# A hybrid SSD and latent-attention step on one core: the page table read whole and early, value weights split a head ahead, values three blocks behind scores, the normalisation later, and long GpSimd products in four pieces

## The chip, the core and the metric

The kernel runs on one core of one Trainium2 chip. The core has five engines with a program each: TensorE (PE; its weight loads, which overlap it, are shown as PEld), VectorE (DVE), ScalarE (ACT), GpSimd (POOL) and SyncE (SP), which issues most of the DMAs. They meet only at semaphores. The metric is the device time of one execution in microseconds (us); less is better.

## What is computed

One inference step of a two-layer decoder trunk: a Mamba-2 layer (SSD), then a multi-head latent attention layer (MLA), each with a residual, and a last RMSNorm. There are two groups of tokens: a prompt of 1024 tokens, and a sample group of 8 sequences with 8 new tokens each and 2048 past tokens in a paged cache. The change lies in the MLA layer, which is cut here to what matters:

```python
def latent_partial(q_lat, q_pe, ckv, kpe, mask):
    s = (einsum('bqhc,bkc->bhqk', q_lat, ckv) + einsum('bqhr,bkr->bhqk', q_pe, kpe)) * MLA_SCALE
    if mask is not None:
        s = where(mask, s, NEG_INF)
    m = max(s, axis=-1)
    p = exp(s - m[..., None])
    return m, sum(p, axis=-1), einsum('bhqk,bkc->bhqc', p, ckv)

# prompt: 16 heads, causal attention of 1024 tokens over themselves
# sample: 8 sequences x 16 pages of 128 tokens, gathered through page_table,
#         running maximum and sum over the pages, then
out = einsum('bhqc,chv->bqhv', acc / l[..., None], w_uv)      # 64 values a head
y   = einsum('bte,ed->btd', out * silu(gate), w_out)
```

Products are done in three passes: each fp32 operand x is split into a rounded half `hi` and the rest `lo = x - hi`, and PE forms hi·hi + lo·hi + hi·lo.

## The kernel before

**Stages.** The SSD layer takes about the first 1090 us and is not touched. Then follow, in the MLA layer: the input products with the gates (to about 1205 us), the latent keys and the query latents (to 1280), the queries `pq` (to 1386), among which head 0's keys, values and maxima are worked in; the sixteen prompt heads (`mla_heads`, 1386 to 1774); and the sample group with the output product (`mla_sample`, to the end). PE and POOL run in the order in which `mla_heads` and `mla_sample` are written; the order of ACT, DVE and SP everywhere, and of all engines before the heads, is chosen by a scheduler that simulates the program. Every engine runs its own list strictly in that order.

**A split** (`split`, L128 to L131) is a copy of the source to `hi` on ACT (L130) and the subtraction `lo` (L131) on DVE, or on POOL where the call says so.

**A head** is 12 blocks of keys by queries (four for the first 512 queries, eight for the second). A block t has scores on PE (`qk`, tile `st`, L1728 to L1735), two exponentials on ACT (`th`, rounded, L1739; `P`, exact, L1740), and `tl = P - th` on POOL, or on DVE for each fourth block (L1742). Its values follow (`pv`, L1759 to L1761: `th` by `Vh`, `th` by `Vl`, `tl` by `Vh`), two blocks later: `held` keeps the blocks between, and `LEAD = 2` sets the distance. Between scores and values stand `units` of preparation: the maxima `sc` of the next head (`maxpass`; DVE takes the maximum), and keys `kp`, queries and values of the head after that (`prep`). After the last block of a half the result is normalised: logarithm and exponential on ACT (`rl`), times the gate on DVE (L1771), times `rl` on POOL (`og`, L1773), and a store.

**Every fourth head** the preparation starts with `prep_group`: the weights of four heads' keys and values are loaded (L1580, L1582; tiles `w`), split with `lo` on POOL, and eight products `vp` with the latents `kvh`, `kvl` make the values `Vh`, `Vl` of four heads. For heads 0 to 3 this happens among the queries.

**The page table.** `gather_kpe` (L1835 on, around 1102 us) reads it as one column `kpidx` and gathers the rotary keys. `Sample.__init__`, which is written after the queries, reads it once more, in four DMAs whose elements of 4 bytes each are copied to 32 partitions (`ptab`, L1866), with a column `pslot` (L1868), and three small DVE instructions (L1870 to L1873) make the row numbers `ptidx` of the latent cache.

**The sample group** goes through 32 steps (8 sequences, 4 groups of 4 pages; `flow`, L2106 on): PE transposes a gathered tile `pgr` (`ct`), forms the scores (`sc`), DVE and ACT the softmax with a running maximum (`mn`, `P`, `ln`), PE transposes `P` (`pt`) and multiplies by the latents' halves `kvh`, `kvl`, DVE adds to the accumulator `ac`. `kvl` is one POOL instruction on 128x1024 elements (L2028). The output product of the prompt (`out.pieces`) is woven into these steps; its weights are split in `weight_split` (L2196 on), with three of the `lo` halves `w5l` on POOL at 128x1024 (L2203), and each of its tiles ends in a scaling of `h` on DVE (L2271). The first 11 steps' worth of `flow` run within the last head.

## Time and profile before

| | us |
|---|---|
| median of three runs (2057.29, 2059.13, 2059.75) | 2059.13 |
| the profiled execution: time | 2057.51 |
| the profiled execution: span of its instructions | 2055.7 |
| PE busy in the span (93%) | 1917.0 |
| DVE, ACT, POOL busy | 1172.9, 1108.1, 826.8 |
| mean granted TensorE clock (1.0 is full) | 0.97 |

The rows of the timeline read: start, duration, engine, line, operation, output<-input with the tiles' names, partitions x elements; in square brackets stands how long the engine was idle before the instruction, and what released it. A line such as `PE vp L89 <- DVE ptf L1871: 17.0, 1, 17.0` is a row of the waits: who waited for whom, total, times, longest.

### The profile page before, as it was taken

What the parts mean: (1) busy time and instruction counts of PE and PEld (TensorE: products, weight loads), DVE (VectorE), ACT (ScalarE), POOL (GpSimd) and SP (SyncE); (2) the same over time, 40 slices, a digit from 0 to 9 for tenths busy, and PEclk for the clock granted to TensorE, in tenths of its full rate; (3) what the DMA queues carried; (4) which work ended last, traced back from release to release, by engine and by line L of the source; (5) the groups of instructions that cost most, each with busy time, mean ns of one, the idle gap of its engine ahead of it and who ended that gap; (6) DMA issues with size and microseconds to landing.
All of it is one profiled execution on the core that took longest, in us unless ns stands there. A gap on an engine that the chain in (4) does not pass through costs nothing.

```text
span 2055.7 us, 33651 instructions
## 1 busy us (share of the span) xinstructions
PE 1917.0 (93%) x11953; PEld 1746.7 (85%) x11953; DVE 1172.9 (57%) x2540; ACT 1108.1 (54%) x2603; POOL 826.8 (40%) x1042
## 2 busy tenths in 40 slices
PE   6989999999999999899999999698989999889998
PEld 5879999999999998777788998697878787678887
DVE  4427675757575666545335134466666666666665
ACT  5446666666666666543335224336667677645552
POOL 0317373636455575331000012005454556755541
PEclk9989999999999999899999999899999999899999
DMA  4113323233333333453446321322111112544441
GB/s 147 41 37 91 91 82 93 88 92 92 90 95 88 87 96 120 163 182 126 172 154 198 142 74 50 97 85 64 43 54 38 43 43 84 159 158 127 145 150 38
DMA packets 186351, 206.43 MB, mean 100 GB/s; under 512 B 23068, under 2 KB 151848, under 8 KB 185800
## 3 DMA queue, kind: packets, MB, share of 16 engines
q1 hardware_dynamic: 181352, 185.27, 29.2%
q0 software_dynamic: 4752, 18.88, 2.8%
q8 instruction: 95, 1.56, 0.3%
q14 instruction: 72, 0.59, 0.1%
q10 hardware_dynamic: 80, 0.13, 0.0%
HBM read 150.92 MB, written 53.15 MB: 99 GB/s over the span
## 4 chain that ended last, share of the span: by engine, by line
PE 70%; DVE 7%; DMA 6%; issue 5%; ACT 5%; POOL 5%; SPq 1%; POOLq 0%; DVEq 0%; ACTq 0%
PE pj L89 21%; PE pj L101 8%; PE pq L101 4%; PE pob L101 4%; PE poa L101 4%; PE py L759 3%; POOL kvl L2028 2%; PE o L1761 1%; PE vp L89 1%; PE pz L101 1%; PE pk L101 1%; DMA tkr<-kpe_dh 1%; PE st L1728 1%; PE p L101 1%; PE st L1729 1%
## 5 line engine op out<-in xcount | busy, mean ns | idle before, releaser
L89 PE MATMUL pj<-xh,wih 128*128 128x384 f32 (+1 forms) x768 | 254.5, 335 | 9.0 <-ACT xh L236 4.6
L89 PE MATMUL pj<-xl,wih 128*128 128x384 f32 (+1 forms) x768 | 254.0, 331 | 0.0
L89 PE MATMUL pj<-xh,wil 128*128 128x384 f32 (+1 forms) x768 | 252.2, 329 | 0.0
L1742 POOL TENSOR_TENSOR tl<-P,th 128x384 fp32r<-128x384 f32 (+1 forms) x144 | 134.4, 941 | 133.2 <-ACT P L1740 109.7
L131 DVE TENSOR_TENSOR wil<-wraw,wih 128x512 fp32r<-128x512 f32 x88 | 70.6, 805 | 160.5 <-ACT wih L130 160.3
L89 PEld LDWEIGHTS pj<-xh,wih 128*128 128x128 f32 x768 | 145.4, 190 | 10.6 <-ACT xh L236 5.6
L89 PEld LDWEIGHTS pj<-xl,wih 128*128 128x128 f32 x768 | 146.0, 190 | 0.6
L89 PEld LDWEIGHTS pj<-xh,wil 128*128 128x128 f32 x768 | 145.7, 190 | 0.0
L796 POOL TENSOR_TENSOR y<-y,xD 128x256 f32<-128x256 f32 x64 | 83.7, 1309 | 151.5 <-DVE y L795 141.1
L1739 ACT ACTIVATE th<-st 128x512 fp32r<-128x512 f32 x192 | 94.2, 491 | 91.4 <-PE st L1735 57.9
L101 PE MATMUL pj<-wih,xh 128*128 128x256 f32 x504 | 143.4, 288 | 0.0
L101 PE MATMUL pj<-wil,xh 128*128 128x256 f32 (+1 forms) x504 | 139.1, 282 | 0.0
L617 DVE SCALAR_TENSOR_TENSOR acc<-raw,vec,acc 128x1112 f32<-128x1112 f32 x84 | 130.3, 1552 | 0.2
L101 PE MATMUL pj<-wih,xl 128*128 128x256 f32 x448 | 126.5, 282 | 0.0
L131 POOL TENSOR_TENSOR xddl<-xdd,xddh 128x256 fp32r<-128x256 f32 x64 | 64.0, 1000 | 117.1 <-ACT xddh L130 117.1
L2028 POOL TENSOR_TENSOR kvl<-pgr,kvh 128x1024 fp32r<-128x1024 f32 x32 | 78.0, 2436 | 75.1 <-ACT kvh L2027 75.1
L130 ACT CAST Ch<-acc 128x128 fp32r<-128x128 f32 x56 | 16.9, 302 | 155.9 <-PE py L89 155.9
L734 ACT ACTIVATE M<-M,tok 128x128 f32<-128x128 f32 (+1 forms) x288 | 90.5, 388 | 10.7 <-DMA M<-acs_d 10.6
L101 PEld LDWEIGHTS pj<-wih,xh 128*128 128x128 f32 x504 | 96.0, 191 | 0.0
L101 PEld LDWEIGHTS pj<-wil,xh 128*128 128x128 f32 (+1 forms) x504 | 93.1, 185 | 0.6
L1740 ACT ACTIVATE P<-st 128x512 f32<-128x512 f32 x192 | 93.2, 486 | 0.0
L1761 PE MATMUL o<-tl,Vh 128*128 128x512 f32 x192 | 71.4, 372 | 17.4 <-POOL tl L1742 14.1
(980 smaller groups left out, 6317.7 us busy)
## 6 DMA issues: line engine op xcount, KB each, us to landing
wraw<-in_ssd_w_in SPq DMA_DIRECT2D x92, 256.0 KB
M<-acs_d SPq DMA_DIRECT2D x64, 256.0 KB
y_d<-xD SPq DMA_DIRECT2D x64, 128.0 KB
s<-in_state_ssm SPq DMA_DIRECT2D x32, 256.0 KB
out_s_ssm<-s SPq DMA_DIRECT2D x32, 256.0 KB
wraw<-in_ssd_w_out SPq DMA_DIRECT2D x16, 512.0 KB
q_d<-qt SPq DMA_DIRECT2D x32, 192.0 KB
qp<-q_d SPq DMA_DIRECT2D x8, 768.0 KB
```

Source lines behind the costliest of these rows:

```text
L89: nc.tensor.matmul(out, a, b, start=(i == 0), stop=(i == n - 1))
L101: nc.tensor.matmul(o, a, b, start=(j == 0), stop=(j == len(ops) - 1))
L131: (eng or nc.vector).tensor_tensor(lo, src, hi.bitcast(F32), op=ALU.subtract)
L617: nc.vector.scalar_tensor_tensor(acc, self.raw[bi][:, j : j + n], k.convw[j][:, blk : blk + 1], acc, op0=ALU.mult, op1=ALU.add)
L734: nc.scalar.activation(M[:m, h, :m], M[:m, h, :m], AF.Relu, bias=c.tk[:, 0, 4 * g + h : 4 * g + h + 1], scale=-1.0)
L759: nc.tensor.matmul(py[:m, h * 64 : h * 64 + 64], c.M[:m, h, :m], c.xdt[:m, h * 64 : h * 64 + 64], start=True, stop=True)
L796: nc.gpsimd.tensor_tensor(y[:m], y[:m], c.xD[:m], op=ALU.add)
L1739: nc.scalar.activation(th[:, :n], ps[:, :n], AF.Exp, scale=SCALE)
L1740: nc.scalar.activation(P[:, :n], ps[:, :n], AF.Exp, scale=SCALE)
L1742: eng.tensor_tensor(tl[:, :n], P[:, :n], th[:, :n].bitcast(F32), op=ALU.subtract)
L1761: nc.tensor.matmul(po[:, o:], va, tl[:, :n], start=False, stop=(jb == nj - 1))
L2028: nc.gpsimd.tensor_tensor(rl, raw, rh.bitcast(F32), op=ALU.subtract)
```

## The change

It has five parts.

1. The page table is read in `gather_kpe`, right behind `kpidx`, in one DMA of the whole table to every partition; four casts pick each quarter's columns, and `ptidx` is made there. `Sample.__init__` only takes it over.
2. The value weights have a function of their own, `prep_v`, called in the preparation of the last head of a group for the next group (for group 0 in `prep_group` as before), and both `lo` halves of the weights are made on DVE.
3. `LEAD` is 3, so that values come three blocks behind scores; `tl` gets a fourth buffer.
4. The last product of the normalisation and its store are put off: `pv` returns them as `close`, which `mla_heads` calls two blocks later.
5. `kvl` and the three `w5l` of POOL are done in four instructions on 128x256 elements each.

```diff
-LEAD = 2
+LEAD = 3
...
+        if h % 4 == 3 and h + 1 < MH:
+            yield from self.prep_v(h // 4 + 1)
 
     def units(self, h):
-        return 4 + 10 * (h % 4 == 0)
+        return 4 + 10 * (h % 4 == 0) + 2 * (h % 4 == 3 and h + 1 < MH)
+
+    def prep_v(self, hg):
+        k, w8 = self.k, self.w8
+        k.nc.sync.dma_start(w8[1], self.wuv[:, 256 * hg : 256 * hg + 256].rearrange("(k p) e -> p k e", p=128))
+        yield
+        split(k, *w8[6:], w8[1])
+        yield
...
-        raw, wv = w8[1], w8[6:]
-        nc.sync.dma_start(raw, self.wuv[:, cs].rearrange("(k p) e -> p k e", p=128))
+        wv = w8[6:]
+        if hg == 0:
+            for _ in self.prep_v(0):
+                pass
         yield
-        split(k, *self.wk, self.wkr, nc.gpsimd)
-        split(k, *wv, raw, nc.gpsimd)
+        split(k, *self.wk, self.wkr)
...
-        tl = sp.tile([128, 512], F32R, tag="tl", name="tl", bufs=3)
+        tl = sp.tile([128, 512], F32R, tag="tl", name="tl", bufs=4)
...
-        nc.gpsimd.tensor_tensor(og[pj], og[pj], rl[pj], op=ALU.mult)
-        nc.sync.dma_start(k.og_d[pr, pj, cs], og[pj])
+        def close():
+            nc.gpsimd.tensor_tensor(og[pj], og[pj], rl[pj], op=ALU.mult)
+            nc.sync.dma_start(k.og_d[pr, pj, cs], og[pj])
+        return close
...
+            if len(closing) and closing[0][0] <= 12 * h + t:
+                closing.pop(0)[1]()
             if len(held) > LEAD:
-                hd.pv(*held.pop(0))
+                c = hd.pv(*held.pop(0))
+                if c:
+                    closing.append((12 * h + t + 2, c))
...
 def gather_kpe(k, pool):
...
+    pt = pool.tile([128, NB * NPG], mybir.dt.int32, name="ptab")
+    nc.sync.dma_start(pt, I["page_table"].rearrange("b p -> (b p)").partition_broadcast(128))
+    ps = pool.tile([128, 1], F32, name="pslot")
+    nc.sync.dma_start(ps, I["c_slot"])
+    pf = pool.tile([128, 32], F32, name="ptf")
+    for j in range(4):
+        r = slice(32 * j, 32 * j + 32)
+        nc.vector.tensor_copy(pf[r], pt[r].rearrange("p (q j) -> p q j", j=4)[:, :, j])
+    nc.vector.tensor_scalar(pf, pf, 32.0, ps, op0=ALU.mult, op1=ALU.add)
+    k.ptidx = k.cm.tile([128, 32], mybir.dt.int32, name="ptidx")
+    nc.vector.tensor_copy(k.ptidx, pf)
...
 class Sample:
     def __init__(self, k, pool):
         nc, I = k.nc, k.I
         self.k, self.sp = k, None
-        pt = pool.tile([128, 32], mybir.dt.int32, name="ptab")
-        for j in range(4):
-            src = I["page_table"].rearrange("b (q j) -> j (b q)", j=4)[j : j + 1].to_broadcast([32, 32])
-            nc.sync.dma_start(pt[32 * j : 32 * j + 32], src)
...
-        self.idx = pool.tile([128, 32], mybir.dt.int32, name="ptidx")
-        nc.vector.tensor_copy(self.idx, pf)
+        self.idx = k.ptidx
...
-        nc.gpsimd.tensor_tensor(rl, raw, rh.bitcast(F32), op=ALU.subtract)
+        for r in range(4):
+            nc.gpsimd.tensor_tensor(rl[:, r], raw[:, r], rh[:, r].bitcast(F32), op=ALU.subtract)
...
-        (nc.gpsimd if x & 2 else nc.vector).tensor_tensor(lo, raw, hi.bitcast(F32), op=ALU.subtract)
+        for c in (slice(256 * j, 256 * j + 256) for j in range(4)) if x & 2 else (slice(0, D),):
+            (nc.gpsimd if x & 2 else nc.vector).tensor_tensor(lo[:, c], raw[:, c], hi[:, c].bitcast(F32), op=ALU.subtract)
```

Lines below `LEAD` are numbered higher in the changed kernel. How the engines' lists change at three places:

DVE among the queries, first before. `cqs` is the scaled query latent of the last (64-token) tile, `cql` its `lo` half, L113 the sum that ends that tile; `qt`, `u`, `w_147..` with `cost` and `sint` are the rotary parts of queries that are stored.

```order
L1459 TENSOR_TENSOR cqs_14663<-cqp_14658,vec 128x512
L1486 TENSOR_TENSOR u_14770<-qt_14755,cost 128x128
L1487 TENSOR_TENSOR w_14771<-qt_14755,sint 128x128
L1488 TENSOR_TENSOR qt_14755<-u_14770,w_14771 128x4x16
L1489 TENSOR_TENSOR qt_14755<-u_14770,w_14771 128x4x16
L1870 CAST ptf<-ptab 128x32
L131 TENSOR_TENSOR cql<-cqs_14663,cqh 128x4x128
L1486 TENSOR_TENSOR u_14792<-qt_14777,cost 128x128
L1487 TENSOR_TENSOR w_14793<-qt_14777,sint 128x128
L1488 TENSOR_TENSOR qt_14777<-u_14792,w_14793 128x4x16
L1489 TENSOR_TENSOR qt_14777<-u_14792,w_14793 128x4x16
L113 TENSOR_TENSOR pq_14684<-pq_14684,pq_14667 64x512
```

The same place after the change, where `w_14736` and `w_14740` are the `lo` halves of the key and value weights:

```order
L1459 TENSOR_TENSOR cqs_14675<-cqp_14670,vec 128x512
L131 TENSOR_TENSOR w_14736<-w_14733,w_14735 128x512
L1486 TENSOR_TENSOR u_14782<-qt_14767,cost 128x128
L1487 TENSOR_TENSOR w_14783<-qt_14767,sint 128x128
L131 TENSOR_TENSOR w_14740<-w_14734,w_14739 128x512
L131 TENSOR_TENSOR cql<-cqs_14675,cqh 128x4x128
L1488 TENSOR_TENSOR qt_14767<-u_14782,w_14783 128x4x16
L1489 TENSOR_TENSOR qt_14767<-u_14782,w_14783 128x4x16
L1486 TENSOR_TENSOR u_14804<-qt_14789,cost 128x128
L1487 TENSOR_TENSOR w_14805<-qt_14789,sint 128x128
L113 TENSOR_TENSOR pq_14696<-pq_14696,pq_14679 64x512
```

The cast of the page table is gone from between `cqs` and `cql`, and two `lo` halves that stood on POOL have come in. The page table's six DVE instructions now stand near 1106 us, here as a piece of the difference (`hl` is the `lo` half of the layer's normalised input, `ck6l` and `ck7l` are weights'):

```order
 L237 SCALAR_TENSOR_TENSOR hl<-xtp_7_12971,vec,hh 128x384
+L1869 CAST ptf<-ptab 32x32 x4
+L1870 TENSOR_SCALAR ptf<-ptf,pslot 128x32
+L1872 CAST ptidx<-ptf 128x32
+L237 SCALAR_TENSOR_TENSOR hl<-xtp_0_13043,vec,hh 128x320
 L131 TENSOR_TENSOR ck6l<-wraw,ck6h 128x288
-L237 SCALAR_TENSOR_TENSOR hl<-xtp_0_13043,vec,hh 128x320
-L131 TENSOR_TENSOR ck7l<-wraw,ck7h 128x288
```

They come ahead of an `hl`, which PE's next products read, and one weight's `lo` half moves behind it.

PE at the start of the heads, before: `o_0` are the values of the first head's first block, `st_0_3` the scores of its fourth, `sc` products for the maxima of the second head.

```order
L1695 MATMUL sc_20_15866<-kTh_14729,qTh_14736 128x384
L1759 MATMUL o_0_15869<-th,Vh_14717 128x512
L1760 MATMUL o_0_15869<-th,Vl_14718 128x512
L1761 MATMUL o_0_15869<-tl,Vh_14717 128x512
L1728 MATMUL st_0_3_15875<-qTh_14733,kTh_13521 128x128
L1729 MATMUL st_0_3_15875<-qTl_14734,kTh_13521 128x128
L1730 MATMUL st_0_3_15875<-qTh_14733,kTl_13522 128x128
L1735 MATMUL st_0_3_15875<-mr 128x128
L1695 MATMUL sc_30_15886<-kTh_14729,qTh_14736 128x512
L1695 MATMUL sc_40_15890<-kTh_14729,qTh_14736 128x512
```

After:

```order
L1704 MATMUL sc_20_15866<-kTh_14741,qTh_14748 128x384
L1737 MATMUL st_0_3_15869<-qTh_14745,kTh_13533 128x128
L1738 MATMUL st_0_3_15869<-qTl_14746,kTh_13533 128x128
L1739 MATMUL st_0_3_15869<-qTh_14745,kTl_13534 128x128
L1744 MATMUL st_0_3_15869<-mr 128x128
L1704 MATMUL sc_30_15880<-kTh_14741,qTh_14748 128x512
L1704 MATMUL sc_40_15884<-kTh_14741,qTh_14748 128x512
L1768 MATMUL o_0_15887<-th,Vh_14729 128x512
L1769 MATMUL o_0_15887<-th,Vl_14730 128x512
L1770 MATMUL o_0_15887<-tl,Vh_14729 128x512
```

The fourth block's scores and two products of the next head's maxima now come ahead of the first values.

POOL in the last head, where the sample group's work starts, before (`tk` is a cast of gathered rotary keys, on 96 partitions):

```order
L1773 TENSOR_TENSOR og_20236<-og_20236,rl_1_20237 64x512
L1742 TENSOR_TENSOR tl<-P,th 128x256
L1742 TENSOR_TENSOR tl<-P,th 128x128
L1945 CAST tk_20297<-tkr_20012 96x512
L2028 TENSOR_TENSOR kvl<-pgr_20008,kvh 128x1024
L1742 TENSOR_TENSOR tl<-P,th 128x512
L1773 TENSOR_TENSOR og_20348<-og_20348,rl_0_20349 64x512
L1742 TENSOR_TENSOR tl<-P,th 128x512 x2
```

After:

```order
L1751 TENSOR_TENSOR tl<-P,th 128x256
L1751 TENSOR_TENSOR tl<-P,th 128x128
L1966 CAST tk_20289<-tkr_20004 96x512
L2050 TENSOR_TENSOR kvl<-pgr_20000,kvh 128x256 x4
L1784 TENSOR_TENSOR og_20256<-og_20256,rl_1_20257 64x512
L1751 TENSOR_TENSOR tl<-P,th 128x512 x3
```

`kvl` is in four, and the `og` of the head before has moved from ahead of two `tl` to behind `kvl`.

More of the change, by code (lines that the diff above doesn't have):

```diff
@@ L1788, in mla_heads @@
     k.tc.keep_in_program_order(k.nc.scalar.preload_act_table_set("natural_log_exp_and_others"))
-    held, carry = [], None
+    held, closing, carry = [], [], None
     def step(g):
@@ L1827, in mla_heads @@
                 step(ready)
+            if len(closing) and closing[0][0] <= 12 * h + t:
+                closing.pop(0)[1]()
             if len(held) > LEAD:
-                hd.pv(*held.pop(0))
+                c = hd.pv(*held.pop(0))
+                if c:
+                    closing.append((12 * h + t + 2, c))
     for x in held:
-        hd.pv(*x)
+        c = hd.pv(*x)
+        if c:
+            closing.append((0, c))
+    for _, c in closing:
+        c()
     return flow
@@ L1862, in __init__ @@
         self.k, self.sp = k, None
-        pt = pool.tile([128, 32], mybir.dt.int32, name="ptab")
-        for j in range(4):
-            src = I["page_table"].rearrange("b (q j) -> j (b q)", j=4)[j : j + 1].to_broadcast([32, 32])
-            nc.sync.dma_start(pt[32 * j : 32 * j + 32], src)
-        ps = pool.tile([128, 1], F32, name="pslot")
-        nc.sync.dma_start(ps, I["c_slot"])
-        pf = pool.tile([128, 32], F32, name="ptf")
-        nc.vector.tensor_copy(pf, pt)
-        nc.vector.tensor_scalar(pf, pf, 32.0, ps, op0=ALU.mult, op1=ALU.add)
-        self.idx = pool.tile([128, 32], mybir.dt.int32, name="ptidx")
-        nc.vector.tensor_copy(self.idx, pf)
+        self.idx = k.ptidx
         self.items = [(b, q) for b in range(NB) for q in range(4)]
```

3 lines of the change are left out of this document (1 added, 2 removed).

## The prediction, made before the changed kernel had run

> **What bounds the kernel.** I read the page's busy times and chain first, then who PE waits for, then the granted clock behind each long wait. The page's rows:
>
> ```profile
> PE 1917.0 (93%) x11953; PEld 1746.7 (85%) x11953; DVE 1172.9 (57%) x2540; ACT 1108.1 (54%) x2603; POOL 826.8 (40%) x1042
> ...
> PE 70%; DVE 7%; DMA 6%; issue 5%; ACT 5%; POOL 5%; SPq 1%; POOLq 0%; DVEq 0%; ACTq 0%
> ```
>
> PE is busy for 1917.0 of 2055.7 us and makes 70% of the chain. No product is added or removed, so the change can only win in PE's 138.7 us of idling, and in the share of its busy time that ran at a low clock. The waits of PE (total, times, longest):
>
> ```profile
> PE vp L89 <- DVE ptf L1871: 17.0, 1, 17.0
> ...
> PE o L1761 <- POOL tl L1742: 14.1, 22, 1.1
> PE vp L89 <- POOL w L131: 9.6, 3, 3.2
> PE pt L2055 <- ACT P L1971: 9.5, 9, 1.3
> ...
> PE act L2086 <- DVE ac L2079: 6.5, 1, 6.5
> ...
> PE o40n L2007 <- ACT pn L2000: 4.4, 1, 4.4
> ```
>
> These are 61.1 us, all in the part that the change touches. Behind the long ones PE also runs slowly. The windows of PE alone (busy time, count, granted clock, DMA share, GB/s) over the stretches that follow them:
>
> ```profile
> 1302.00:1308.00 6.00, 5.69 (x28) 0.66 0.42 143
> 1391.00:1403.00 12.00, 9.88 (x31) 0.57 0.25 72
> 1440.00:1450.00 10.00, 9.45 (x47) 0.70 0.19 53
> 1535.00:1545.00 10.00, 9.17 (x44) 0.67 0.19 54
> 1631.00:1641.00 10.00, 9.33 (x46) 0.69 0.11 28
> 1759.00:1769.00 10.00, 9.13 (x36) 0.61 0.40 99
> 1787.00:1797.00 10.00, 9.20 (x39) 0.66 1.02 293
> 1808.00:1818.00 10.00, 8.90 (x36) 0.67 0.43 159
> ```
>
> Busy time by one less the clock is what full speed would have saved: 1.9, 4.2, 2.8, 3.0, 2.9, 3.6, 3.1 and 2.9 us, 24.4 in all. A wait of 3 us thus costs about 6.
>
> The Trainium skill ("TensorE: Matmul & The Clock Gate", Part 1) has the clock halve after an idle window of about 3.4 us, the window running freely. By that figure the three stalls of 3.2 us need not cost any clock, and the sum below would be 8.7 us smaller; the three windows at 1440, 1535 and 1631 show 0.67 to 0.70, so the rows decide.
>
> **Page table: 17.5 us gained.** Rows of the chain, of DVE and of PE:
>
> ```profile
> 1280.64 19.24 DMA ptab<-in_page_table
> ```
>
> ```profile
> 1280.51 0.68 DVE L1459 TENSOR_TENSOR cqs<-cqp,vec 128x512 f32<-128x512 f32 x1
> ...
> 1300.00 0.18 DVE L1870 CAST ptf<-ptab 128x32 f32<-128x32 int32 x1 [18.02 <-DMA ptab<-in_page_table]
> 1300.09 0.69 DVE L131 TENSOR_TENSOR cql<-cqs,cqh 128x512 fp32r<-128x512 f32 x1
> ```
>
> ```profile
> 1302.31 0.77 PE L89 MATMUL vp<-w,kvh 128*128 128x256 f32 x2 [16.99 <-DVE ptf L1871]
> ```
>
> DVE stood 18.02 us at a cast that nothing nearby needs, and `cql` and the sum of L113, which frees a PSUM buffer for `vp`, stood behind it. In the new order that cast is gone and two weight halves (0.69 each, as `cql`) are in. From `cqs` at 1280.5 DVE then has about seven steps to L113, which ends near 1285.0 (an estimate: three more halves at 0.6 and four rotary steps at 0.2 after `cqs`, then L113 at 0.6); PE came free at 1285.3 (1302.31 less 16.99). So the whole 17.0 and the 1.9 of clock go, less what the new place costs:
>
> ```profile
> 1102.08 0.42 SPq L1838 DMA_DIRECT2D kpidx<-in_page_table  x1
> ```
>
> ```profile
> 1106.39 1.28 POOL L1840 DMA_INDIRECT kprows<-in_cache_kpe,kpidx  x1 [11.24 <-DMA kpidx<-in_page_table]
> ```
>
> ```profile
> 1108.46 0.46 DVE L131 TENSOR_TENSOR ck6l<-wraw,ck6h 128x288 fp32r<-128x288 f32 x1 [1.61 <-ACT ck6h L130]
> ```
>
> There `kpidx`, issued just ahead of the new DMAs, had landed by 1106.4, and DVE idled 1.61 us before 1108.46, so six casts of 0.2 fit in. Two more DMAs go through SP, at 0.4 each ahead of weight loads. If the table is late by some us, `hl` is late: I take 1.4 off, with 0 and 5 as the ends. Gain 17.5, from 14 to 19.
>
> **Value weights: 17 us gained.** The weights' halves on POOL:
>
> ```profile
> 1438.01 2.49 POOL L131 TENSOR_TENSOR w<-w,w 128x512 fp32r<-128x512 f32 x2
> ```
>
> POOL makes them only when `vp` is due, 1.27 each. Made a head ahead, on DVE at 0.69, they are there; the key weights' half has eight `vp` before `kp` needs it. That takes away 9.6 of waits and 2.8 + 3.0 + 2.9 of clock, 18.3. Against it stand eight halves on DVE, 5.5 us among 375 in which DVE is busy for 242.55 (row below). Gain 17, from 15 to 18.
>
> **Three blocks instead of two: 12 us gained.** The heads' window (PE, PEld, DVE, ACT, POOL), and the product that is put off:
>
> ```profile
> 1370.00:1745.00 375.00, 343.55 (x1915) 295.24 (x1915) 242.55 (x627) 245.21 (x542) 187.87 (x203) 0.96 0.19 54
> ```
>
> ```profile
> L1773 POOL TENSOR_TENSOR og<-og,rl 64x512 f32<-64x512 f32 x32 | 41.1, 1285 | 43.3 <-ACT rl L1772 30.0 <-PE sc L1695 4.8 <-PE pt40n L1998 2.7
> ```
>
> A block is worth 2.0 us (375 by 192). The 22 waits for `tl` are 1.1 at most, so one more block covers each, and POOL no longer waits 30.0 us for `rl` with `tl` behind it. No engine is full there. Gain 12 of 14.1, from 8 to 13.5; the rest is the last head and the start, below.
>
> **The start of the heads: 1 us lost.** The fourth block and two `sc` now come ahead of the first values. Before:
>
> ```profile
> 1392.31 0.80 PE L1761 MATMUL o<-tl,Vh 128*128 128x512 f32 x1 [2.81 <-DVE tl L1742]
> ...
> 1394.55 0.77 PE L1695 MATMUL sc<-kTh,qTh 96*128 96x512 f32 x1 [0.16 <-DVE kTl L131]
> ```
>
> ```profile
> 1392.17 0.29 DVE L1700 CUSTOM_DVE_ANT_0 sc<-sc,mk 128x128 f32<-128x128 f32 x1
> ```
>
> One would think that 0.5 us of `st` and the `sc` fill the 2.81. But four buffers of `sc` are taken by then (`sc_00`, `sc_10`, `kp`, `sc_20`), and the next comes free with the mask at 1392.17, the one after with `kTl` by 1394.5, on the same late DVE. So PE stops at `sc` about as long, the clock still drops, and it gets to the first values only behind `sc_40`. I take a loss of 1, from a loss of 3 to a gain of 2.
>
> **Four pieces on POOL: 11.5 us gained in three places.** A DVE operation with two inputs waits for a running POOL one:
>
> ```profile
> 1749.22 4.90 DVE L1742 TENSOR_TENSOR tl<-P,th 128x512 fp32r<-128x512 f32 x1 [1.61 <-ACT P L1740]
> ```
>
> ```profile
> 1749.34 0.60 POOL L1945 CAST tk<-tkr 96x512 fp32r<-96x512 f32 x1
> 1749.92 2.39 POOL L2028 TENSOR_TENSOR kvl<-pgr,kvh 128x1024 fp32r<-128x1024 f32 x1
> 1752.28 1.29 POOL L1742 TENSOR_TENSOR tl<-P,th 128x512 fp32r<-128x512 f32 x1
> ```
>
> ```profile
> 1898.21 2.39 POOL L2028 TENSOR_TENSOR kvl<-pgr,kvh 128x1024 fp32r<-128x1024 f32 x1
> ```
>
> ```profile
> 1898.26 3.55 DVE L2271 SCALAR_TENSOR_TENSOR h<-h,ss,fw 128x512 f32<-128x512 f32 x2 [0.69 <-POOL ss L2264]
> ```
>
> The price of the pieces: between these rows (mean ns of one).
>
> ```profile
> L2028 POOL TENSOR_TENSOR kvl<-pgr,kvh 128x1024 fp32r<-128x1024 f32 x32 | 78.0, 2436 | 75.1 <-ACT kvh L2027 75.1
> ...
> L1742 POOL TENSOR_TENSOR tl<-P,th 128x256 fp32r<-128x256 f32 x32 | 23.3, 730 | 15.1 <-PE qT L1643 8.7 <-ACT P L1740 4.2 <-PE ql7p L1666 0.3
> ```
>
> Four quarters by 730 are 2.92 against 2.44: at most 0.5 us more an instruction, 17 for 35, on an engine half idle; at the least nothing. (1) In the steady steps the two scalings of `h` take 3.55, while two of its size need 1.3 (0.69 each, as `cql`). With pieces DVE can enter after the first (0.6) and then take turns: 2.6, so 0.95 earlier in six or so of the nine waits at `pt`. Gain 5.5, from 0 to 7.4. (2) Around 1800, `ac` is late because DVE's halves of the output weights wait for POOL likewise, the last of them right ahead of it:
>
> ```profile
> 1805.72 2.97 DVE L2203 TENSOR_TENSOR w5l<-w5r,w5h 128x1024 fp32r<-128x1024 f32 x1
> ```
>
> PE's 6.5 should shrink by about 3, while the clock stays low. What comes earlier there is a load, as the chain has it:
>
> ```profile
> 1784.88 8.36 DMA tkr<-kpe_dh
> ```
>
> Nothing moves that. Gain 3, from 0 to 3.5. (3) At the flow's start, 4.4 of wait and 3.6 of clock hang on the `tl` of 4.90; the new POOL order there is longer (`kvl` in four, then `og`, then three `tl`). Gain 3, from a loss of 4 to 7.5.
>
> The Trainium skill ("SBUF — State Buffer", on the port that DVE and GpSimd share) calls that port an exclusive lock which an instruction holds to its end while the other blocks. Taken by the instruction, `tl` should have entered at 1749.92 or 1752.28 at the latest, and (3) would give its 7.5; the row of 4.90 ran through both ends, so I take less than half. By the page's rule the sum would be 4.5 us better.
>
> **Sum.** 17.5 + 17 + 12 - 1 + 5.5 + 3 + 3 = 57 us. From the profiled execution's 2057.5 (span 2055.7 and 1.8 around it) that leaves 2000.5. The median of the runs is 2059.13, 1.6 above the profiled one, so I say **2002**.
>
> **Rivals.** (a) *The pieces give nothing*: DVE stays shut out until POOL has run dry, as in the row of 4.90, across four pieces as across three instructions. Then the 11.5 are 0, or 4 are lost: 2002 + 11.5 to 15.5, about 2015. For it speaks that one row; against it that `h` is met by pieces of equal shape on all partitions. (b) *The heads give back*: with 12 blocks a head, another wait ends last (the `sc` buffers, `nm`, DVE with its eight halves), and of the 12 + 17 only the 8.7 of clock and half of the waits (22) remain: 2002 + 9.5, about 2012; with (a) 2025. Against it: no engine but PE is busy for over 66% there. (c) *The wait moves with the table*: if the new read takes as long as the old (19.24 us from issue), DVE stands from 1107 to about 1123 with `hl` behind it, and most of the 17.5 is gone: about 2018. Against it: the old one copies 4096 elements of 4 bytes, the new one 128 whole rows, and `kpidx` landed in 4 us. (d) *Slower*: POOL's run of pieces keeps DVE's `mn` and `ln`, which sit in every step's softmax, out for the whole run, in all 32 steps. To be slower it must eat the other 45.5, that is 1.4 us of PE in each step; the run grows by 0.5 at most, so it would have to fall on `mn` in steps where it doesn't now. At 1.6 us a step it gives 2002 + 11.5 + 51, about 2065.
>
> **Chances.** Forecast with its own range 1990 to 2009: 62%. (a) or (b) or both, 2009 to 2029: 25%. (c): 5%. (d): 3%. A sum of these that comes out within 0.2% of before: 2%. Better than 1990: 3%. The best ends add to 19 + 18 + 13.5 + 2 + 7.4 + 3.5 + 7.5 = 70.9, the worst to 14 + 15 + 8 - 3 + 0 + 0 - 4 = 30; so 1988 to 2029, which leaves out about 1 in 10. A measurement tells a difference of 0.2% (4 us) from none: faster 95%, same 2%, slower 3%.
>
> **What would show it.** In the changed profile: no wait of `vp` on `ptf` or on `w`, and full clock at 1308 of the old scale; the row of PE for `tl` under 3 us; at the heads' start a wait of 2 to 3 us at `sc`, not at `tl`, with the clock low; `h` twice in about 2.6; PE's `act` wait near 3.5. It is wrong if DVE shows a long idle before the casts of the table near 1107, if a new row of over 10 us stands among PE's waits, or if `kvl` takes over 3 us in its four pieces.

## The result, and the profile after

The changed kernel takes 1994.6 us (median of 4 runs, 1993.71 to 1995.32) against 2058.21 for the one before (4 runs, 2054.48 to 2059.75): a ratio of 0.9693, 95% interval 0.9677 to 0.971. The forecast was 2002, within 1988 to 2029; 57 us were forecast and some 64 came.

The page of the changed kernel's profile (span 1991.9 us) has these lines on busy time and on the chain that ended last:

```profile
PE 1899.0 (95%) x11953; PEld 1739.5 (87%) x11953; DVE 1179.2 (59%) x2551; ACT 1108.6 (56%) x2603; POOL 844.9 (42%) x1142
...
PE 85%; DMA 4%; DVE 4%; ACT 4%; issue 2%; SPq 1%; POOL 0%; POOLq 0%; DVEq 0%; ACTq 0%
```

PE is idle for 92.9 us instead of 138.7, and its busy time is 18.0 us shorter with the same number of products (clock, and more below); the chain is PE's for 85% instead of 70%. The waits of PE in the part that the change touches (who for whom: total, times, longest):

```profile
PE pt L2077 <- ACT P L1992: 7.9, 7, 4.7
PE act L2108 <- ACT cTh L130: 4.4, 1, 4.4
PE o L1770 <- POOL tl L1751: 3.2, 1, 3.2
PE sc L1704 <- DVE mx L1709: 2.8, 1, 2.8
PE sc L89 <- POOL tk L1966: 2.7, 1, 2.7
PE nmp L1719 <- DVE nm L1716: 1.8, 5, 0.5
PE o40n L2028 <- ACT pn L2021: 1.7, 1, 1.7
```

The 17.0 for `ptf`, the 9.6 for `w` and the waits for `tl` are gone but for one, in the fifteenth head, which has grown from 0.2 to 3.2. New is the wait of `sc` at the heads' start; the flow's start and the stretch near 1730 to 1750 (`pt`, `tk`, `act`) still stop PE.

To see which stage gained, four moments are read from PE's timeline in each profiled execution: the fourth `o<-tl` (the fourth block of values of the first head), the first `ct`, the 65th `ct` (the ninth of the 32 steps of the sample group), and the end. The count starts at the first `vp`, near 1282, since the first layer is not touched and its length differs by up to 4 us between these executions. All runs below are put in this way, in us gained on the kernel before, from its profiled execution.

| kernel | to the heads' fourth block | heads | flow's start | steady steps | sum | median of runs |
|---|---|---|---|---|---|---|
| all five parts (the change) | 19.2 | 36.1 | 3.5 | 5.1 | 63.9 | 1994.6 |
| page table alone | 19.2 | -0.3 | 1.1 | 0.3 | 20.3 | 2036.5 |
| value weights alone | 0.6 | 18.4 | 3.2 | -0.1 | 22.2 | 2035.6 |
| lead of three alone | -0.9 | 14.9 | 3.6 | -0.1 | 17.5 | 2037.6 |
| delayed product alone | -1.6 | 11.0 | 7.4 | 0.1 | 16.9 | 2038.4 |
| pieces alone | 0.1 | -2.9 | -1.0 | 5.1 | 1.3 | 2056.0 |
| the change without the lead | 18.5 | 25.9 | 0.3 | 5.3 | 50.0 | 2005.7 |
| the change without the pieces | 18.3 | 33.7 | 6.6 | 0.3 | 58.8 | 1996.5 |

The first moment is the fourth block and not the first, because a lead of three puts a block of scores and two `sc` ahead of the first values, so that these come later with nothing lost. A stage of one execution is good to a few us only: up to the first `ct`, before any piece has run, the kernels with and without the pieces have the same lists on all engines, and yet the columns differ by 2.8 (the pieces alone against before) and 3.4 (the change with and without them).

### The profile page after: what moved, and what is told of

It is laid out like the page before. It is cut to its first block, busy times and chain, and to the rows that moved or that the text cites. A ratio compares the mean times of both kernels' runs of the same rounds, so it can differ in the third digit from the quotient of the medians.

```text
span 1991.9 us, 33767 instructions
## 1 busy us (share of the span) xinstructions
PE 1899.0 (95%) x11953; PEld 1739.5 (87%) x11953; DVE 1179.2 (59%) x2551; ACT 1108.6 (56%) x2603; POOL 844.9 (42%) x1142
## 4 chain that ended last, share of the span: by engine, by line
PE 85%; DMA 4%; DVE 4%; ACT 4%; issue 2%; SPq 1%; POOL 0%; POOLq 0%; DVEq 0%; ACTq 0%
PE pj L89 23%; PE pj L101 9%; PE pq L101 5%; PE p L101 5%; PE pob L101 4%; PE poa L101 4%; PE py L759 3%; PE sc L89 2%; PE o L89 2%; PE sc L1704 1%; PE o L1770 1%; PE st L1737 1%; PE o L1769 1%; PE st L1738 1%; PE o L1768 1%
## 5 line engine op out<-in xcount | busy, mean ns | idle before, releaser
L2050 POOL TENSOR_TENSOR kvl<-pgr,kvh 128x256 fp32r<-128x256 f32 x128 | 98.9, 800 | 53.4 <-ACT kvh L2048 53.4
L130 ACT CAST Ch<-acc 128x128 fp32r<-128x128 f32 x56 | 16.9, 302 | 153.7 <-PE py L89 153.7
L101 PEld LDWEIGHTS pj<-wih,xl 128*128 128x128 f32 x448 | 85.6, 191 | 0.0
```

The source lines that it names most:

```text
L101: nc.tensor.matmul(o, a, b, start=(j == 0), stop=(j == len(ops) - 1))
L2050: nc.gpsimd.tensor_tensor(rl[:, r], raw[:, r], rh[:, r].bitcast(F32), op=ALU.subtract)
```

## Experiments

**One part alone** (four kernels, timed together; before is 2056.6 there).

The page table, its two hunks on the kernel before:

```diff
 def gather_kpe(k, pool):
...
+    pt = pool.tile([128, NB * NPG], mybir.dt.int32, name="ptab")
+    nc.sync.dma_start(pt, I["page_table"].rearrange("b p -> (b p)").partition_broadcast(128))
...
-            nc.sync.dma_start(pt[32 * j : 32 * j + 32], src)
...
+        self.idx = k.ptidx
```

> Before, with the page table's part of the change alone. The prediction's term: 17.5 us gained (14 to 19), all between the first vp and the heads' start: the wait of vp on ptf (17.0) is gone, no wait over 1 us appears near 1107 us, and nothing else moves; 2058.2 - 17.5 = about 2040.7. Rival (the wait moves with the table): DVE idles over 5 us ahead of the casts near 1107 and less than 14 us is gained.

2036.5 us, ratio 0.9902 (0.9886 to 0.9919): about 20 us, a little over the range of 14 to 19. The new place costs nothing that shows: PE's listed waits between 1085 and 1280 add to 2.6 before and to 1.5 here. DVE in the changed kernel there:

```profile
1105.85 1.09 DVE L1869 CAST ptf<-ptab 32x32 f32<-32x32 int32 x4
1106.97 0.24 DVE L1870 TENSOR_SCALAR ptf<-ptf,pslot 128x32 f32<-128x32 f32 x1
1107.24 0.18 DVE L1872 CAST ptidx<-ptf 128x32 int32<-128x32 f32 x1
```

No bracket stands in the first row: the table was there when DVE came. And at the old place the sum of L113 comes in time for `vp`, as worked out (1284.07 and 0.68 long, then PE without a stop; the rows are DVE's and PE's):

```profile
1284.07 0.68 DVE L113 TENSOR_TENSOR pq<-pq,pq 64x512 f32<-64x512 f32 x1
```

```profile
1285.22 0.28 PE L89 MATMUL vp<-w,kvh 128*128 128x256 f32 x1
```

The value weights: `prep_v`, the call in `prep`, `units`, and both splits on DVE, as in the change.

```diff
+        if h % 4 == 3 and h + 1 < MH:
+            yield from self.prep_v(h // 4 + 1)
...
-        split(k, *self.wk, self.wkr, nc.gpsimd)
-        split(k, *wv, raw, nc.gpsimd)
+        split(k, *self.wk, self.wkr)
```

> Before, with the value weights' part alone (split a head ahead, on DVE). The prediction's term: 17 us (15 to 18), in three steps of about 6 at heads 4, 8 and 12; about 2041. If each stop of PE costs more than the waits' row says (the tail of the product ahead of it, about 0.2 us), 18 or 19. If eight more halves on DVE cost something, as the rival had it, under 14, with new waits for DVE in the heads.

2035.6 us, 0.9892 (0.9876 to 0.9909): 21 us. 18.4 of it stand in the heads, about 6 at each of the three groups, and 3 at the flow's start, which were not followed up.

The lead and the fourth `tl` buffer:

```diff
-LEAD = 2
+LEAD = 3
...
-        tl = sp.tile([128, 512], F32R, tag="tl", name="tl", bufs=3)
+        tl = sp.tile([128, 512], F32R, tag="tl", name="tl", bufs=4)
```

> Before, with values three blocks behind scores and four tl buffers alone; the normalisation's product still stands where it stood. The prediction's terms: 12 for the waits on tl less 1 at the start: 11, about 2047. In the changed kernel the heads gained 40 us where 29 were forecast. If the waits' rows understate each stop by the tail of the product ahead (0.2 us) the lead alone gives about 16 to 18, about 2041. If the delayed product did part of it, 11 or less, and waits on tl behind og stay.

2037.6 us, 0.9904 (0.9888 to 0.9921): 19 us. The heads' first values came 4.2 later, but by the fourth block only 0.9 of that is left, with a block of scores more already done. In the heads from there on no wait for `tl` was left. The term of 12 was too small.

The pieces:

```diff
-        nc.gpsimd.tensor_tensor(rl, raw, rh.bitcast(F32), op=ALU.subtract)
+        for r in range(4):
+            nc.gpsimd.tensor_tensor(rl[:, r], raw[:, r], rh[:, r].bitcast(F32), op=ALU.subtract)
...
-        (nc.gpsimd if x & 2 else nc.vector).tensor_tensor(lo, raw, hi.bitcast(F32), op=ALU.subtract)
+        for c in (slice(256 * j, 256 * j + 256) for j in range(4)) if x & 2 else (slice(0, D),):
+            (nc.gpsimd if x & 2 else nc.vector).tensor_tensor(lo[:, c], raw[:, c], hi[:, c].bitcast(F32), op=ALU.subtract)
```

> Before, with the long POOL products in four pieces alone. The prediction's terms: 11.5 us (5.5 in the steady steps, 3 near 1800, 3 at the flow's start); about 2047. The changed kernel gained 8 us from the last head to the end, all parts together: by that, 8. Rival (a), DVE stays shut out: 0 or a loss of up to 4, h twice still 3.5. My theory now: pieces let DVE in when no operation on fewer than 128 partitions ran just ahead on POOL, and not behind tk (96 partitions): h twice in about 2.6, but w5l and ln of DVE still over 2.5 us near 1800.

2056.0 us, 0.9996 (0.9987 to 1.0006): nothing in sum, but not in its places. The steady steps gained 5.1. What stands on DVE there, from the groups of before and of the changed kernel (mean ns of one behind the total):

```profile
L2271 DVE SCALAR_TENSOR_TENSOR h<-h,ss,fw 128x512 f32<-128x512 f32 x16 | 24.5, 1570 | 4.8 <-POOL ss L2264 4.8
```

```profile
L2294 DVE SCALAR_TENSOR_TENSOR h<-h,ss,fw 128x512 f32<-128x512 f32 x16 | 17.0, 1104 | 4.8 <-POOL ss L2287 4.8
```

7.5 us less over eight tiles, 0.94 each: the 0.95 of the forecast (with the pieces alone the mean is 1106). PE's waits at `pt` in these steps go from 7.4 us (6 times, 1.3 at most) to 2.6 (5 times, 0.5 at most) with the pieces alone. At the flow's start, DVE's `tl` got worse instead. DVE and POOL with the pieces alone:

```profile
1751.11 5.32 DVE L1742 TENSOR_TENSOR tl<-P,th 128x512 fp32r<-128x512 f32 x1 [1.61 <-ACT P L1740]
```

```profile
1750.15 1.14 POOL L1742 TENSOR_TENSOR tl<-P,th 128x256 fp32r<-128x256 f32 x2
1751.24 0.60 POOL L1945 CAST tk<-tkr 96x512 fp32r<-96x512 f32 x1
1751.82 2.81 POOL L2029 TENSOR_TENSOR kvl<-pgr,kvh 128x256 fp32r<-128x256 f32 x4
1754.59 1.27 POOL L1742 TENSOR_TENSOR tl<-P,th 128x512 fp32r<-128x512 f32 x1
```

Six ends of POOL operations passed, four of them pieces, and DVE came in only when POOL ran dry. Rival (a) is what happens here, and the opposite of it in the steady steps. Its price is less clear. The stage shows 1.0 lost behind the first `ct`; the 2.9 of the heads were lost before the first piece ran, where ACT's `kvh` waited 0.5 us longer for a gather and PE's clock then halved for 6.8 us, which can't be the pieces' doing. By the medians of ten and thirteen runs, which differ by 0.5, some 4.5 should be lost outside the steady steps, give or take 2; where, stays open.

**The delayed product alone** (timed with the two kernels that change `tk` alone and the one on the heads' start, further down; before is 2056.9).

```diff
-        nc.gpsimd.tensor_tensor(og[pj], og[pj], rl[pj], op=ALU.mult)
-        nc.sync.dma_start(k.og_d[pr, pj, cs], og[pj])
+        def close():
+            nc.gpsimd.tensor_tensor(og[pj], og[pj], rl[pj], op=ALU.mult)
+            nc.sync.dma_start(k.og_d[pr, pj, cs], og[pj])
+        return close
...
+                if c:
+                    closing.append((12 * h + t + 2, c))
```

> Before, with the delayed product of the normalisation alone, values still two blocks behind. The lead alone took all 22 waits of PE on tl and gave 18.9 us. If the waits came from og standing ahead of tl on POOL, this part alone takes most of them too: 8 to 14 us, about 2046. My theory: they come from the time that exponentials and tl take after scores, which only the lead covers: 0 to 4 us, about 2055, and the 22 waits stay.

2038.4 us, 0.9909 (0.9892 to 0.9925): 18 us, as much as the lead alone; my expectation was a miss. With the old lead of two the waits for `tl` in the heads are gone but for two: one of 0.6 at the heads' start, as before, and one in the fifteenth head that has grown from 0.2 to 5.3 (the waits of PE in the heads):

```profile
PE vp L89 <- POOL w L131: 9.6, 3, 3.2
PE o L1761 <- POOL tl L1742: 6.0, 2, 5.3
PE nmp L1710 <- DVE nm L1707: 5.4, 6, 1.3
```

So the waits came from `og`, which stood on POOL ahead of `tl` and waited there for `rl`. A block more of distance covers that, and taking `og` away removes it. The stop of 5.3 is the delayed product's own: the lead alone has none there.

**What the lead does beside the delayed product.** The change with `LEAD` 2 and three `tl` buffers, and, timed with it (before 2057.2), the change with `kvl` and `w5l` whole.

```diff
-LEAD = 3
+LEAD = 2
...
-        tl = sp.tile([128, 512], F32R, tag="tl", name="tl", bufs=4)
+        tl = sp.tile([128, 512], F32R, tag="tl", name="tl", bufs=3)
```

> After, with values two blocks behind scores again (and three tl buffers); the rest of the change stays. Alone the lead gave 18.9 us and the delayed product 18.5, and the five parts alone add to 79 where all give 62 to 64. Theory: lead and delayed product free the same waits on tl, so either will do; without the lead the kernel is 2 to 3 us slower in the heads and 2.6 faster at their start: 1992 to 1998. Rival: the lead is what counts and the sum fails elsewhere: 2005 or more, with waits on tl back (10 or more of them).

2005.7 us, 0.9748 (0.9731 to 0.9764): 11 us slower than the change. Neither expectation holds: the waits for `tl` are not back, but the lead is not superfluous. PE came 2.7 us earlier to the first values, but 0.7 later to the fourth block. The loss is mostly in other places: a stretch at half clock in the second head that followed two waits of 0.79 and 0.43 (3.4 us), 1.7 in all over the ten heads from the fourth to the thirteenth, and the fifteenth head, where POOL's delayed `og` waits and the `tl` behind it with it:

```profile
1688.91 0.79 PE L1770 MATMUL o<-tl,Vh 128*128 128x512 f32 x1 [5.28 <-POOL tl L1751]
```

```profile
1686.26 1.26 POOL L1784 TENSOR_TENSOR og<-og,rl 64x512 f32<-64x512 f32 x1 [4.55 <-ACT P L1749]
```

In the change that stop is 3.2, behind an `og` that waited likewise (POOL):

```profile
1677.17 1.26 POOL L1784 TENSOR_TENSOR og<-og,rl 64x512 f32<-64x512 f32 x1 [4.34 <-DVE og L1780]
```

The pieces undone:

```diff
-        for r in range(4):
-            nc.gpsimd.tensor_tensor(rl[:, r], raw[:, r], rh[:, r].bitcast(F32), op=ALU.subtract)
+        nc.gpsimd.tensor_tensor(rl, raw, rh.bitcast(F32), op=ALU.subtract)
...
+        (nc.gpsimd if x & 2 else nc.vector).tensor_tensor(lo, raw, hi.bitcast(F32), op=ALU.subtract)
```

> After, with kvl and w5l in one POOL instruction each again. Alone the pieces gave 0.5 us: 5 gained in the steady steps, 4 lost where the flow starts, 1 near 1800. If the parts add, 1995 to 1996; if the loss at the flow's start was only met without the lead (there DVE's tl waits 2.15 in the changed kernel, not 5.32), 1998 to 2001. The steady steps (from the transposes of the 9th item to the end) take 5 us longer than in the changed kernel either way.

1996.5 us, 0.9703 (0.9687 to 0.9719), which the interval can't tell from the change's 0.9693. By the stages the pieces bring 4.8 in the steady steps and lose 3.1 at the flow's start. The 3.4 that the change has more up to the first `ct` are not theirs, as said at the table.

**Why DVE is shut out at some ends and not at others.** DVE and POOL hold each other up without any semaphore. Near 1738 the changed kernel has it at its worst (DVE, then POOL):

```profile
1738.58 5.35 DVE L2226 TENSOR_TENSOR w5l<-w5r,w5h 128x1024 fp32r<-128x1024 f32 x1 [2.51 <-ACT w5h L2224]
```

```profile
1736.31 1.06 POOL L1972 DMA_INDIRECT pgr<-in_cache_ckv,ptidx  x1 [0.16 <-POOL w5l L2226]
1737.38 0.62 POOL L1966 CAST tk<-tkr 96x512 fp32r<-96x512 f32 x1
1737.96 2.79 POOL L2226 TENSOR_TENSOR w5l<-w5r,w5h 128x256 fp32r<-128x256 f32 x4
1740.72 3.80 POOL L2050 TENSOR_TENSOR kvl<-pgr,kvh 128x256 fp32r<-128x256 f32 x4
```

Four pieces take 2.79 where DVE got nothing in between, and 3.80 where its operation of 1.2 came in, ahead of the last piece. Over these traces I counted each two-input operation of DVE that started while POOL ran and took over 0.25 us longer than the shortest of its kind, and asked whether it came in at the first end of a POOL operation that another followed within 0.1 us. Where POOL had run nothing but operations on 128 partitions since its last pause, it always did. Where a gather, or an operation on fewer partitions (`tk` 96, `og` 64, `qpr` 32), was among them, it often did not.

The first test fills `tk` to 128 partitions, by loading one part of the rotary keys a second time; the product still reads 96:

```diff
-        self.tkr = self.ep.tile([96, 4, 256], F32, tag="tkr", name=f"tkr{n}", bufs=1)
-        for j in range(3):
+        self.tkr = self.ep.tile([128, 4, 256], F32, tag="tkr", name=f"tkr{n}", bufs=1)
+        for j in range(4):
...
-        tk = self.ep.tile([96, 4, 128], F32R, tag="tk", name=f"tk{n}", bufs=2)
+        tk = self.ep.tile([128, 4, 128], F32R, tag="tk", name=f"tk{n}", bufs=2)
...
-            (k.qpr[:, b], self.tk.pop(n))])
+            (k.qpr[:, b], self.tk.pop(n)[:96])])
```

> After, with the cast tk on all 128 partitions of POOL instead of 96 (its tile loads one part of the rotary keys twice to fill them; the product reads 96 as before). Theory: behind an operation on 96 partitions the POOL operations that follow without a pause never leave DVE a gap (w5l 5.35 us and ln 3.30 in the changed kernel, tl 5.32 with the pieces alone), so with full ones DVE enters after at most one piece: no w5l or ln of DVE over 2.6 us, PE's waits of 4.7, 2.7 and 4.4 near 1730 to 1750 shrink by 3 to 6 in all, about 1990. Rival: the port goes to POOL's next operation whatever its partitions: w5l stays over 4 us somewhere, and the time is the same or 1 to 2 us longer for the fourth load: 1995 to 1997.

1994.5 us, 0.969 (0.9674 to 0.9706): no change, and DVE's `w5l` still took 4.44, past four ends of pieces. The 96 partitions of `tk` are not needed for it. A gather stands right ahead of `tk` in that run, however.

`tk` on ACT instead:

```diff
 def RT(nc):
-    return nc.gpsimd.tensor_copy
+    return nc.scalar.copy
```

> After, with the cast tk on ACT instead of POOL. By the theory of the partitions the long waits of DVE go as with 128 partitions, w5l and ln of DVE under 2.6 us, and PE no longer waits for POOL's tk (2.7): 1988 to 1992. By the rival they stay, and 32 casts of 0.6 us come ahead of exponentials on ACT: 1996 to 2003.

1988.6 us, 0.9661 (0.9645 to 0.9677): 6 us better than the change, as expected, but not for the reason expected. With no `tk` on POOL, DVE's `ol` (a half of the same size as `w5l`) was held longest of all, behind a gather (POOL and DVE):

```profile
1731.91 1.92 POOL L1972 DMA_INDIRECT pgr<-in_cache_ckv,ptidx  x1
1733.86 2.78 POOL L2226 TENSOR_TENSOR w5l<-w5r,w5h 128x256 fp32r<-128x256 f32 x4
1736.61 3.78 POOL L2050 TENSOR_TENSOR kvl<-pgr,kvh 128x256 fp32r<-128x256 f32 x4
```

```profile
1733.81 5.99 DVE L131 TENSOR_TENSOR ol<-og,oh 128x1024 fp32r<-128x1024 f32 x1 [0.43 <-ACT oh L130]
```

What it gained is PE's wait for `tk` on POOL (2.7 in the change), and waits at `pt`, 7.9 in the change and 3.5 here.

`tk` on ACT, and the gathers at the end of a step:

```diff
-            if n >= 0 and n + PRE < N:
-                self.load(n + PRE)
...
             if t:
                 self.halves(n + 1)
...
+            if n >= 0 and n + PRE < N:
+                self.load(n + PRE)
             yield
```

> After, with the cast tk on ACT and POOL's gathers issued at the end of a step, behind kvl, so that no gather and no operation on fewer than 128 partitions runs just ahead of the pieces w5l and kvl. Over ten traces DVE operations that met a running POOL operation entered at its end in all 544 cases in which nothing but full operations had run since POOL's last pause, and missed 90 ends in 279 cases where a gather or an operation on fewer partitions was among them. Theory (those leave the cores of POOL out of step): no DVE operation of the sample group waits over 1.0 us, ol and w5l under 2.3 us where the kernel with tk on ACT alone had 5.99; 2 to 4 us faster than that one (1988.6): about 1985.5. Rival (the pieces that stand queued lock the port, whatever ran ahead): waits over 2.5 us stay, 1988 or more.

1986.1 us, 0.9662 (0.9645 to 0.9678): no operation of DVE in the sample group took over 0.9 us longer than the shortest of its kind, and the stages show 71.0 gained against 66.7 for `tk` on ACT alone, though the medians of the two are within their intervals. It proves less than it should: next to `w5l` a gather still stands right ahead of a run of eight pieces, and DVE's `w5l` came into that run only when one piece was left to start. In the kernel below an operation of DVE came early in it, and was held.

**The heads' start, and a better version.** The third and fourth keys' rotary rows (DVE) and constant rows (POOL) were moved into the first head:

```diff
-        for a, b in self.kT:
+        for a, b in self.kT[:2]:
             nc.gpsimd.memset(a[96:98].bitcast(F32), 1.0)
...
+            if h == 0 and 6 <= t < 10:
+                if t == 6:
+                    rest = hd.later()
+                next(rest, None)
```

> After, with the rotary rows and constant rows of the third and fourth key buffers, and the constants of the second value buffer, written in the middle of the first head instead of ahead of it, and the mask first. The waits of PE at the heads' start (2.85, 1.22 and 0.98, with 2.5 of clock) are said to come from these casts on DVE and fills on POOL ahead of the first tl and mask. By that the start gains 4 to 7 us: about 1989. Rival: they come from the DMA that the reused memory waits for (the stored queries, the mask): less than 2 us, about 1993 to 1995.

1998.9 us, 0.9718 (0.9702 to 0.9734): 4 us slower. It tells nothing about the casts, since the scheduler put them ahead of the first `tl` all the same (DVE):

```profile
1369.27 1.20 DVE L1553 CAST kTl<-kTl 32x1024 fp32r<-32x1024 f32 x1
1370.50 0.83 DVE L1770 TENSOR_TENSOR tl<-P,th 128x512 fp32r<-128x512 f32 x1
```

PE still stopped for 3.22 us at `sc`, and the fills that now stood among POOL's `tl` held up DVE's `nm` for 3.4 us a few blocks on. What sets the start is left open.

The last kernel takes the one with the gathers at the end of a step, and adds the old distance in the first four blocks and one more block for the delayed product:

```diff
-            if len(held) > LEAD:
+            if len(held) > (LEAD if h or t > 3 else 2):
...
-                    closing.append((12 * h + t + 2, c))
+                    closing.append((12 * h + t + 3, c))
```

> The kernel with tk on ACT and the gathers behind kvl (1986.1), with two changes of mla_heads: in the first four blocks of the first head values come two blocks behind scores as before, and the delayed product is put off by three blocks instead of two. Theory of the start: the order with the lead of three costs 2.2 us there (the kernel with the rest of the change but the old lead reached the first values 2.2 us earlier), so that much comes back and the stop is again at tl. In the last head POOL's og, which waited 4.3 us for rl, stands ahead of the tl for which PE then waits 3.3 us with 1.7 of clock; behind it, that stop goes: 3 to 5 us. Together 1979 to 1982. If the start's stop is set by the late DVE in either order: 0 there, and 1981 to 1983.

1985.3 us, 0.9646 (0.9633 to 0.966): the fastest of all by its median, but not told apart from the 1986.1. The old distance gained nothing: PE's first values came 2.5 us earlier than with the gathers moved alone, at a stop of 2.63 for `tl` as before the change, but the third block came 0.8 later. The delayed product did what it was for: the stop of 3.3 in the fifteenth head became two of 0.8 and 1.4, and the heads gained 2.9. But 5.9 us were lost again between the sixth step and the ninth. The row of DVE:

```profile
1741.30 5.10 DVE L2096 SCALAR_TENSOR_TENSOR ln<-l41n,f,l 128x1 f32<-128x1 f32 x1 [1.12 <-ACT f L1996]
```

`ln` has one column, and PE waited 5.1 us for `ac`, which DVE makes from it. POOL did eight pieces behind a gather then, and paused only at 1746.4:

```profile
1738.94 1.91 POOL L1972 DMA_INDIRECT pgr<-in_cache_ckv,ptidx  x1 [0.16 <-POOL kvl L2050]
1740.88 2.79 POOL L2226 TENSOR_TENSOR w5l<-w5r,w5h 128x256 fp32r<-128x256 f32 x4
1743.63 2.76 POOL L2050 TENSOR_TENSOR kvl<-pgr,kvh 128x256 fp32r<-128x256 f32 x4
```

## Why the prediction was right, point by point

**Page table: 17.5 forecast, 19.2 measured alone.** The mechanism was right in each step: the casts out of the way, L113 in time by 0.5 us, nothing late at the new place. The 1.4 taken off for the new place was not needed. (Ahead of L113 the new list has six rotary steps where the prediction counts four, and the steps that it names add to 1284.4, not 1285.0; L113 ended at 1284.75.)

**The heads' start: -1 forecast, between 0 and -1.** The mechanism was right, word for word. In the changed kernel PE stops at `sc`, not at `tl` (PE, then DVE):

```profile
1373.41 0.80 PE L1704 MATMUL sc<-kTh,qTh 96*128 96x512 f32 x1 [2.85 <-DVE mx L1709]
1375.43 0.76 PE L1704 MATMUL sc<-kTh,qTh 96*128 96x512 f32 x1 [1.22 <-DVE kTl L131]
```

```profile
1372.40 0.69 DVE L1751 TENSOR_TENSOR tl<-P,th 128x512 fp32r<-128x512 f32 x1
1373.01 0.29 DVE L1709 CUSTOM_DVE_ANT_0 sc<-sc,mk 128x128 f32<-128x128 f32 x1
1373.22 0.14 DVE L1709 DVE_READ_ACCUMULATOR2_ANT mx<- 128x1 f32 x1
```

The first values alone would tell another size: they came 4.2 later with the lead alone, and 3.7 later in the change than with the page table alone. But of the first block's three products two used to stand ahead of the stop, and now all come behind it, and the fourth block's scores and two `sc` are done before them. By the fourth block of values the change has gained 19.2, as the page table alone has, and the lead alone has lost 0.9, with a block of scores more done in both.

**Value weights: 17 forecast, 18.4 measured in the heads.** Waits of 9.6 and clock of 8.7 went as summed; the 1.3 for eight halves on DVE was not paid.

**Three blocks and the delayed product: 12 forecast, 17.7 measured** (36.1 from the fourth block to the first `ct`, less 18.4). This is the term that was mis-sized, from 8 to 13.5. The windows of PE between those two moments (length, busy time, count, clock, DMA share, GB/s), before and after:

```profile
1402.57:1743.10 340.53, 312.69 (x1764) 0.97 0.18 50
```

```profile
1383.39:1687.80 304.41, 298.29 (x1756) 0.99 0.20 55
```

Idle time fell by 21.7 us, from 27.8 to 6.1; of this 9.6 are the value weights', so 12.1 are the `tl` and smaller waits: the 12. Busy time fell by 14.4, and some 6 of that is clock (0.03 of 312.69 against 0.01 of 298.29), the value weights' 8.7 less what a new half-clock stretch behind the stop of 3.2 costs. The rest, some 8 us, the forecast had not seen: about 2 are eight products fewer in the second window, 4 come from how a wait is counted, and 2 are left unexplained. Two rows of before, ahead of the stop at the heads' start:

```profile
1388.87 0.40 PE L1759 MATMUL o<-th,Vh 128*128 128x512 f32 x1
1389.11 0.40 PE L1760 MATMUL o<-th,Vl 128*128 128x512 f32 x1
```

The second starts 0.24 after the first, though each is shown as 0.40 long: products overlap. A stop is counted from the end of the product ahead of it, so a stop costs 0.16 more than its row says. Of the 31 stops of over 0.2 us in that window six are left, and 25 by 0.16 are 4 us. The step that failed is "12 of 14.1": it took the rows of the waits for the price of the stops.

The reason given, that one more block covers each wait and that `og` no longer stands ahead of `tl`, named two causes as one. The runs part them: the waits are those of `og` for `rl`, either part removes them, and together they give 17.7 where each alone gives 11.0 and 14.9 in the heads. Overlooked was what the delay costs: in the fifteenth head the `og` that was put off comes to stand ahead of other `tl`, and makes the new stop of 3.2.

**Steady steps: 5.5 forecast, 5.1 measured**, by the mechanism stated (two `h` took 3.1 by the groups' mean, and take 2.2, and the waits at `pt` shrank by 4.8).

**Flow's start and near 1800: 6 forecast from the pieces; they lost about 1 there alone and 3 in company**, as far as single executions show. Here the weighing was wrong: I took less than half of what the first end would give, when the row of 4.90 had shown a run in which no end gave anything. That the stretch gained 3.5 in the change comes from the other parts; alone, the value weights, the lead and the delayed product gain 3.2, 3.6 and 7.4 there. Rival (a) held there; its price of up to 4 fits, but is not measured closer than that.

Rivals (b), (c) and (d) did not come. Not all the signs did either: the row of PE for `tl` is 3.2 and not under 3, `act` waits 4.4 and not 3.5 (for ACT's `cTh`), and `kvl` takes 3.3 to 3.8 in 10 of its 32 runs of four pieces, which was named a sign of being wrong. It takes 2.8 otherwise; the longer ones have an operation of DVE among them, most of them the `h` that was to come in, so the sign was badly chosen.

The errors had opposite signs: by the stages the heads gave 36.1 where 29 were forecast, the way to them 19.2 for 16.5, the flow's start 3.5 for 6, the steady steps 5.1 for 5.5; so 57 stood beside 64. That the total lies well inside its range, with one term above its best end and the pieces at the flow's start a loss, is in part luck.

## What to carry to other kernels

A wait of PE costs its row, plus the overlap of the product ahead of it, plus the clock behind it; with many short stops the second adds up (4 us here). Look first for an instruction that waits in order ahead of work that is due (the page table's cast, `og` ahead of `tl`, a weight's half when its product is due): moving that one was worth nearly 60 of the 64 us, though the table is also read in another way and the weights' halves are made on another engine. Two parts that each free the same wait are not to be added, a moment by which stages are parted must have the same work behind it in both kernels, and cutting a long GpSimd operation helps the engine beside it only where POOL's ends really let it in, which is to be read from the rows at the place itself.

## What the runs showed of the hardware that was not expected

Over the fourteen profiled executions (kinds of operation told apart by line, tiles and shape; told apart otherwise the totals shift, and the ends missed in the first group stay none), DVE's two-input operations that met a running POOL operation and found another following came in at its end in 880 of 880 cases when POOL had done only operations on 128 partitions since its last pause. Where a gather or an operation on fewer partitions was among them, 125 of 184 missed at least one end, and up to seven in a row. These are not so many independent cases: 756 of the 880 and 98 of the 125 are the same places of the first layer, met again in each execution. The 98 lie behind an operation on 96 partitions with no gather in the run, and all of them missed; with gathers alone 4 of 7 did, and behind `og` alone (64 partitions) 9 of 52. So either can be enough, and neither always is.

The Trainium skill ("SBUF — State Buffer", on the shared port) calls the port a lock that is held for the whole instruction; by that rule an instruction's end is where the other may enter. The 880 agree with it and the 125 do not, at least not if each piece counts as an instruction of its own. Why such an operation ahead shuts DVE out, and why some do and others don't, stays open.

The clock halved after stops of 2.6 to 2.9 us (the heads' start in the change and in the last kernel), and once behind two stops of 0.79 and 0.43 with 2.0 us between them (the change without the lead).
